# Dropping the empty slots' rows from the experts' indirect transfers, and adding their results to the residual by accumulating transfers on GpSimd's queue

## The chip, the cores and the metric

The kernel runs on one core of one Trainium2 chip. The metric is device time in microseconds (us) of one execution; lower is better. The engines are called PE (TensorE, matrix products), PEld (its weight loads), DVE (VectorE), ACT (ScalarE), POOL (GpSimd) and SP (SyncE, which here only issues transfers). SPq and POOLq are the queues of transfers that SP and POOL issue.

## The reference

Two blocks of layers run one behind the other on a sequence of 256 tokens of 1024 numbers. The change lies in one layer of the first block, a mixture of eight experts of which each token takes two:

```python
N_EXPERTS = 8
TOP_K = 2
D_FF_EXPERT = 7 * D_MODEL // 2
...
def moe_swiglu(xn, router, w_gu, w_down):
    logits = (xn @ router).astype(jnp.float32)
    top_v, top_i = lax.top_k(logits, TOP_K)
    w = jax.nn.softmax(top_v, axis=-1)
    comb = jnp.sum(jax.nn.one_hot(top_i, N_EXPERTS, dtype=jnp.float32) * w[..., None],
                   axis=-2).astype(xn.dtype)
    out = jnp.zeros_like(xn)
    for e in range(N_EXPERTS):
        out = out + comb[..., e:e + 1] * swiglu(xn, w_gu[e], w_down[e])
    return out
```

The layer's result is added to the residual: `h = h + moe_swiglu(rmsnorm(h, od_norm_moe[i]), od_router[i], ...)`. All tensors are float32.

## The kernel before

Weights come from DRAM in units of 1 MB (128 x 2048 float32, four blocks of 128 x 512). SP issues each as one transfer into one of four buffers `raw`. ACT casts each half to a rounded form `wh` (line 395), DVE forms the rest `wl = raw - wh` (line 396), and PE multiplies with both parts (line 372), three products for each block: `xh*wh`, `xl*wh`, `xh*wl`. There are five buffers of `wh` and four of `wl`, each half a unit. SP issues the next unit when DVE is through with the oldest `raw`. A unit is twelve products of 128 x 512, and the program is written in a fixed order; a tile framework's scheduler orders each engine's queue and sets the semaphores.

An expert holds 128 slots. Token t that goes to expert e has the slot that is its rank among the expert's tokens, so slots are filled from 0 upward (`pick` compares the rank with an iota). 256 tokens with two experts each make 512 filled slots of 8 x 128 = 1024: half are empty on average. A second pass for experts with more than 128 tokens stands in a branch and isn't taken here.

For expert e (`expert`, line 1260) the rows of its tokens are gathered from DRAM by slot (`slots`, an indirect transfer of 128 rows of 4 KB into `mo_got`, line 1245), transposed on PE and split (`turn`). Seven steps j follow, each of two products (gate, up), of 8 blocks each; ACT's `ff_s` at line 1281 stands once in each step, behind the gate's product. Two halves n of the down product follow, of 28 blocks each. Each half is scaled by the token's weight into `mo_y` (line 1294) and written by an indirect transfer of 128 rows of 2 KB to a DRAM tensor `results[n]` (named `mo_res`, line 1295): row t for a token whose first choice the expert is, row 256 + t for a second choice, and a spare row 512 + slot for an empty slot. `clear_results` sets the first 512 rows to zero early in the program. An empty slot's gather index is 0.

The last expert's results don't take that way: they are multiplied back to token order on PE and added to the residual `res` by DVE (line 1305). Ahead of that the other seven experts' results are collected (`collect`, at steps j = 2 and 3 of the last expert): for each half n and each choice w, SP loads 256 rows of 2 KB into `mo_z` (line 1326) and POOL adds them to `res` (line 1329, two instructions of 128 x 512 each, eight in all).

POOL runs its queue in order, the issuing of its transfers included.

Of the kernel before, what the change touches and what calls it, by code (L numbers as in the profile page):

```python
# [7 lines left out]
F32 = mybir.dt.float32  # L8
# [8 lines left out]
S = 256  # L17
# [6 lines left out]
TAPS_PE = 20  # L24
POOL_WINDOWS = (2, 4, 8, 16)
HQ = 64

# [65 lines left out]
def prep(i):  # L93
# [109 lines left out]
    slot = 2 * S + np.arange(128, dtype=np.float32)  # L203
    a["spare"] = np.stack([slot, -slot], axis=1)
    a["bigrows"] = np.ascontiguousarray(np.stack([f["final_norm"], f["od_norm_moe"][0], f["od_pw2_b"][0]]))

    p = np.arange(128)
# [96 lines left out]
class Build:  # L304
# [909 lines left out]
    def slot_tables(self, e):  # L1214

        nc = self.nc
        v = nc.vector
        P = self.picked  # L1220
        cws, rws, cw = self.slot_factors(e, P, self.moe_state[2])
        if e < NE - 1:
            to = self.sm(1, "mo_to")
            f = self.sm(NE + 1, "mo_to")
            v.tensor_copy(f, cw[:, NE + 2:])
            v.scalar_tensor_tensor(to, f[:, :1], self.spare[:, 1:2], f[:, 1 + e:2 + e], ALU.mult, ALU.add)
            back = self.sm(1, "mo_tx", I32)
            v.tensor_tensor(back, to, self.spare[:, 0:1], ALU.add)
        else:
            tr = self.scp(256)  # L1230
            for b in range(2):
                self.tp(tr[:, b * 128:b * 128 + 128], P[:, b])
            back = self.keep(S, "mo_PT", F32R)
            nc.scalar.copy(back, tr)
        return back, cws, rws, cw[:, NE + 1:NE + 2]

    def slots(self, e):


        nc = self.nc  # L1240
        back, cws, rws, at = self.slot_tables(e)
        ix = self.sm(1, "mo_ix", I32)
        nc.vector.tensor_copy(ix, at)
        got = self.sm(D, "mo_got")
        nc.gpsimd.indirect_dma_start(got, None, self.moe_state[1], bass.IndirectOffsetOnAxis(ap=ix.bitcast(U32), axis=0))
        return got, back, cws, rws

    def turn(self, slots):
# [11 lines left out]
    def expert(self, e, rest, then=None):  # L1260
# [29 lines left out]
        for n in range(2):  # L1290
            py, = self.ts(xh, xl, "moe_down", base + n * DFE * 512, DFE // 128, nb=1)
            if not then:
                y = self.sm(512, "mo_y")
                nc.scalar.activation(y, py, AF.Copy, scale=cws)
                nc.gpsimd.indirect_dma_start(self.results[n], bass.IndirectOffsetOnAxis(ap=back.bitcast(U32), axis=0), y, None)
                continue
            yh = self.sm(512, "mo_yh", F32R)
            yl = self.sm(512, "mo_yl", F32R)
            self.split_gain(yh, yl, py, cws)
            for b in range(2):  # L1300
                po = self.scp(512)
                self.mm(po, back[:, b * 128:b * 128 + 128], yh, True, False)
                self.mm(po, back[:, b * 128:b * 128 + 128], yl, False, True)
                r = self.res[b][:, n * 512:n * 512 + 512]
                v.tensor_tensor(r, po, r, ALU.add)
            then.half(n)

    def clear_results(self):
# [2 lines left out]
        nc = self.nc  # L1311
        zero = self.sm(512, "mo_zero")
        nc.gpsimd.memset(zero, 0.0)
        self.results = [self.dram.tile([2 * S + 128, 512], F32, name=f"mo_res{n}") for n in range(2)]
        for y in self.results:
            nc.scalar.dma_start(y[:2 * S].rearrange("(a p) d -> p a d", p=128), zero.unsqueeze(1).to_broadcast([128, 4, 512]))

        self.spare = self.keep(2, "mo_sp")
        nc.sync.dma_start(self.spare, self.A["spare"])

    def collect(self, n):

        nc = self.nc
        for w in range(2):
            z = self.sm((2, 512), "mo_z")
            nc.sync.dma_start(z, self.results[n][w * S:w * S + S].rearrange("(b p) d -> p b d", p=128))
            for b in range(2):
# [772 lines left out]
```

## Time and profile before

| | |
|---|---|
| time, median of 3 runs | 2287.48 us (2286.06 to 2288.99) |
| time of the profiled execution | 2284.27 us |
| its span, first to last instruction | 2282.4 us |
| mean granted TensorE clock | 0.999 |
| busy: PE, PEld, DVE, ACT, POOL | 2252.5, 1935.2, 1798.6, 1444.3, 115.1 us |
| bytes moved, mean rate | 588.63 MB, 258 GB/s |

The profiled execution lies 3.2 us (0.14%) below the median of the runs; about 1.9 us of it lie outside its span. Busy time of PE counts matrix products whose ends are modelled, so a high share doesn't say that PE runs at its peak. The eight experts run from about 616 us to 1611 us of the span.

### The profile page before, as it was taken

What the parts mean: (1) busy time and instruction counts of PE and PEld (TensorE: products, weight loads), DVE (VectorE), ACT (ScalarE), POOL (GpSimd) and SP (SyncE); (2) the same over time, 40 slices, a digit from 0 to 9 for tenths busy, and PEclk for the clock granted to TensorE, in tenths of its full rate; (3) what the DMA queues carried; (4) which work ended last, traced back from release to release, by engine and by line L of the source; (5) the groups of instructions that cost most, each with busy time, mean ns of one, the idle gap of its engine ahead of it and who ended that gap; (6) DMA issues with size and microseconds to landing.
All of it is one profiled execution on the core that took longest, in us unless ns stands there. A gap on an engine that the chain in (4) does not pass through costs nothing.

```text
span 2282.4 us, 34629 instructions
## 1 busy us (share of the span) xinstructions
PE 2252.5 (99%) x13069; PEld 1935.2 (85%) x13069; DVE 1798.6 (79%) x2601; ACT 1444.3 (63%) x2005; POOL 115.1 (5%) x163
## 2 busy tenths in 40 slices
PE   8999999999999999999999999989999999999999
PEld 8999998888878788888788878867788998888997
DVE  7656656986698898889898989888877885876883
ACT  5555545466567777777777777767765544665542
POOL 2100001301000000000000000020000000000000
PEclk9999999999999999999999999999999999999999
DMA  7544755954599989999999999989623555513553
GB/s 280 194 152 166 252 192 203 265 186 162 184 365 354 379 346 368 360 388 360 388 368 381 362 376 366 378 345 346 226 74 119 197 190 177 181 56 131 199 179 120
DMA packets 90891, 588.63 MB, mean 258 GB/s; under 512 B 11232, under 2 KB 12512, under 8 KB 24032
## 3 DMA queue, kind: packets, MB, share of 16 engines
q1 hardware_dynamic: 84752, 570.20, 67.7%
q0 software_dynamic: 4048, 12.97, 1.9%
q10 hardware_dynamic: 1920, 3.22, 0.4%
q8 instruction: 103, 1.69, 0.3%
q14 instruction: 68, 0.56, 0.1%
HBM read 577.31 MB, written 9.04 MB: 257 GB/s over the span
## 4 chain that ended last, share of the span: by engine, by line
PE 64%; DMA 4%; DVE 3%; ACT 1%; issue 1%; POOL 0%; ACTq 0%; DVEq 0%; POOLq 0%
PE acc L372 59%; DMA raw<-in_moe_gu_dram 3%; PE tr L376 3%; DVE wl L396 2%; PE sc L372 2%; ACT wh L395 1%; DMA raw<-in_moe_down_dram 0%; DMA ahead<-in_moe_gu_dram 0%; PE tr L372 0%; DVE res L556 0%; DVE xl L400 0%; POOL res L2043 0%; ACT at_p L1805 0%; DVE ff_s L1282 0%; DVE at_nm L1801 0%
## 5 line engine op out<-in xcount | busy, mean ns | idle before, releaser
L396 DVE TENSOR_TENSOR wl<-raw,wh 128x1024 fp32r<-128x1024 f32 x1054 | 1258.0, 1227 | 305.1 <-PE acc L372 176.9
L395 ACT CAST wh<-raw 128x1024 fp32r<-128x1024 f32 x1054 | 1060.1, 1047 | 431.5 <-PE acc L372 342.0
L372 PE MATMUL acc<-wh,mo_g 128*128 128x512 f32 x1568 | 488.8, 393 | 2.4 <-ACT wh L395 2.4
L372 PE MATMUL acc<-xl,wh 128*128 128x256 f32 x1440 | 399.1, 277 | 3.3 <-DVE xl L400 3.3
L372 PE MATMUL acc<-xh,wh 128*128 128x256 f32 x1440 | 399.7, 279 | 0.9 <-ACT xh L399 0.8
L372 PE MATMUL acc<-xh,wl 128*128 128x256 f32 x1440 | 398.0, 277 | 0.4 <-DVE wl L396 0.4
L372 PEld LDWEIGHTS acc<-wh,mo_g 128*128 128x128 f32 x1568 | 295.3, 189 | 64.8 <-ACT wh L395 3.5
L372 PE MATMUL acc<-wl,mo_g 128*128 128x512 f32 x784 | 314.8, 401 | 5.4 <-DVE wl L396 5.2
L372 PEld LDWEIGHTS acc<-xl,wh 128*128 128x128 f32 x1440 | 270.5, 188 | 5.2 <-DVE xl L400 4.5
L372 PEld LDWEIGHTS acc<-xh,wh 128*128 128x128 f32 x1440 | 270.0, 188 | 2.0 <-ACT xh L399 1.7
L372 PEld LDWEIGHTS acc<-xh,wl 128*128 128x128 f32 x1440 | 270.6, 188 | 0.6 <-DVE wl L396 0.6
L372 PEld LDWEIGHTS acc<-wl,mo_g 128*128 128x128 f32 x784 | 147.6, 188 | 49.4 <-DVE wl L396 21.4
L372 PE MATMUL acc<-wl,mhh 128*128 128x512 f32 x448 | 178.7, 399 | 2.4 <-DVE wl L396 1.6
L372 PE MATMUL acc<-wh,mhl 128*128 128x512 f32 x448 | 176.1, 393 | 0.0
L372 PE MATMUL acc<-wh,mhh 128*128 128x512 f32 x448 | 175.3, 391 | 0.0
L372 PEld LDWEIGHTS acc<-wl,mhh 128*128 128x128 f32 x448 | 84.2, 188 | 25.5 <-DVE wl L396 8.7
L372 PE MATMUL acc<-wl,hh 128*128 128x512 f32 x264 | 104.0, 394 | 0.0
L372 PE MATMUL acc<-wh,hl 128*128 128x512 f32 x264 | 103.5, 392 | 0.0
L372 PE MATMUL acc<-wh,hh 128*128 128x512 f32 x264 | 102.8, 390 | 0.0
L372 PEld LDWEIGHTS acc<-wh,mhl 128*128 128x128 f32 x448 | 84.1, 188 | 18.4
L372 PEld LDWEIGHTS acc<-wh,mhh 128*128 128x128 f32 x448 | 84.3, 188 | 17.2
L395 ACT CAST mhh<-tr 128x512 fp32r<-128x512 f32 x56 | 32.9, 588 | 94.8 <-PE tr L376 94.8
(439 smaller groups left out, 3103.8 us busy)
## 6 DMA issues: line engine op xcount, KB each, us to landing
raw<-in_moe_gu_dram SPq DMA_DIRECT2D x222, 1024.0 KB, 7.0
raw<-in_moe_down_dram SPq DMA_DIRECT2D x112, 1024.0 KB, 6.1
raw<-in_gu_dram SPq DMA_DIRECT2D x66, 1024.0 KB, 4.9
raw<-in_down_dram SPq DMA_DIRECT2D x30, 1024.0 KB, 4.8
raw<-in_w_in_b_dram SPq DMA_DIRECT2D x20, 1024.0 KB, 5.0
raw<-in_wkv_dram SPq DMA_DIRECT2D x16, 1024.0 KB, 5.0
raw<-in_pw_dram SPq DMA_DIRECT2D x12, 1024.0 KB, 4.8
raw<-in_wq_dram SPq DMA_DIRECT2D x8, 1024.0 KB, 4.8
```

What stands on the lines that cost most here:

```text
L372: self.nc.tensor.matmul(out, lhsT=l, rhs=r, start=start, stop=stop)
L376: self.nc.tensor.transpose(out, in_, self.ident[:n, :n])
L395: self.nc.scalar.copy(h, src)
L396: self.nc.vector.tensor_tensor(l, src, h.bitcast(F32), ALU.subtract)
```

## The change

The gather and the result writes get a bound: an index above it is skipped. An empty slot's index becomes 4096 (`PAST`) in both tables, so its row is neither read nor written; the spare rows of `mo_res`, the table `spare` and its load go away. DVE forms both indices in one pair of instructions, where it formed the write index in three and the gather index in one of its own. `collect` is called once, at step j = 0 of the last expert: eight transfers from DRAM on POOL's queue, each 128 rows of 2 KB, which the transfer itself adds to `res`. The loads into `mo_z` and POOL's eight additions go away.

```diff
+PAST = 4096.0
...
-    a["spare"] = np.stack([slot, -slot], axis=1)
...
         cws, rws, cw = self.slot_factors(e, P, self.moe_state[2])
+        f = self.sm(NE + 2, "mo_f")
+        v.tensor_copy(f, cw[:, NE + 1:])
         if e < NE - 1:
-            to = self.sm(1, "mo_to")
-            f = self.sm(NE + 1, "mo_to")
-            v.tensor_copy(f, cw[:, NE + 2:])
-            v.scalar_tensor_tensor(to, f[:, :1], self.spare[:, 1:2], f[:, 1 + e:2 + e], ALU.mult, ALU.add)
-            back = self.sm(1, "mo_tx", I32)
-            v.tensor_tensor(back, to, self.spare[:, 0:1], ALU.add)
...
+            to = self.sm(2, "mo_to")
+            v.scalar_tensor_tensor(to, f[:, 1:2].to_broadcast([128, 2]), -PAST, f[:, 0:3 + e:2 + e], ALU.mult, ALU.add)
+            ix = self.sm(2, "mo_tx", I32)
+            v.tensor_scalar(ix, to, PAST, None, ALU.add)
+            return ix[:, 1:2], cws, rws, ix[:, 0:1]
...
-        ix = self.sm(1, "mo_ix", I32)
-        nc.vector.tensor_copy(ix, at)
         got = self.sm(D, "mo_got")
-        nc.gpsimd.indirect_dma_start(got, None, self.moe_state[1], bass.IndirectOffsetOnAxis(ap=ix.bitcast(U32), axis=0))
+        nc.gpsimd.indirect_dma_start(got, None, self.moe_state[1], bass.IndirectOffsetOnAxis(ap=ix.bitcast(U32), axis=0),
+                                     bounds_check=S - 1, oob_is_err=False)
...
-            if e == NE - 1 and j in (2, 3):
-                self.collect(j - 2)
+            if e == NE - 1 and j == 0:
+                self.collect()
...
-                nc.gpsimd.indirect_dma_start(self.results[n], bass.IndirectOffsetOnAxis(ap=back.bitcast(U32), axis=0), y, None)
+                nc.gpsimd.indirect_dma_start(self.results[n], bass.IndirectOffsetOnAxis(ap=back.bitcast(U32), axis=0), y, None,
+                                             bounds_check=2 * S - 1, oob_is_err=False)
...
-    def collect(self, n):
...
-        for w in range(2):
-            z = self.sm((2, 512), "mo_z")
-            nc.sync.dma_start(z, self.results[n][w * S:w * S + S].rearrange("(b p) d -> p b d", p=128))
-            for b in range(2):
-                r = self.res[b][:, n * 512:n * 512 + 512]
-                nc.gpsimd.tensor_tensor(r, r, z[:, b], ALU.add)
...
+    def collect(self):
+
+        for n in range(2):
+            for w in range(2):
+                for b in range(2):
+                    r = self.res[b][:, n * 512:n * 512 + 512]
+                    row = (2 * w + b) * 128
+                    self.nc.gpsimd.dma_start(r, self.results[n][row:row + 128], accum_op=ALU.add)
```

POOL's queue at the change from the seventh expert to the last, before (`mo_res_2946` and `mo_res_2947` are the two halves n of the results, `res_69` and `res_70` the two row blocks of the residual):

```order
L1245 DMA mo_got<-mo_rows,mo_ix 128x1024
L1295 DMA mo_res_2946<-mo_y,mo_tx 640x512
L1295 DMA mo_res_2947<-mo_y,mo_tx 640x512
L1329 TENSOR_TENSOR res_69<-res_69,mo_z 128x512
L1329 TENSOR_TENSOR res_70<-res_70,mo_z 128x512
```

The four rows of line 1329 that follow, twice this pair and then another, read alike. The same place of POOL's queue in the changed kernel:

```order
L1244 DMA mo_got<-mo_rows,mo_tx 128x1024
L1295 DMA mo_res_2946<-mo_y,mo_tx 512x512
L1326 DMA res_69<-mo_res_2946 128x512
L1326 DMA res_70<-mo_res_2946 128x512
L1326 DMA res_69<-mo_res_2946 128x512
L1326 DMA res_70<-mo_res_2946 128x512
L1295 DMA mo_res_2947<-mo_y,mo_tx 512x512
L1326 DMA res_69<-mo_res_2947 128x512
L1326 DMA res_70<-mo_res_2947 128x512
L1326 DMA res_69<-mo_res_2947 128x512
L1326 DMA res_70<-mo_res_2947 128x512
```

Eight additions have become eight transfers. The four of the first half stand ahead of the seventh expert's second result write; the second choice's pair stands behind the first choice's and adds to the same tiles.

SP's queue over the last expert, before:

```order
L473 DMA raw<-in_moe_gu_dram 128x2048 x11
L1326 DMA mo_z<-mo_res_2946 128x2x512 x2
L473 DMA raw<-in_moe_gu_dram 128x2048 x5
L1326 DMA mo_z<-mo_res_2947 128x2x512 x2
L473 DMA raw<-in_moe_gu_dram 128x2048 x12
L473 DMA raw<-in_moe_down_dram 128x2048 x8
```

And in the changed kernel:

```order
L472 DMA raw<-in_moe_gu_dram 128x2048 x28
L472 DMA raw<-in_moe_down_dram 128x2048 x8
```

The four loads between the units of weights are gone; the units stand in the same order.

## Rows read from the trace of the kernel before

**Rows 1.** The page: the chain of work that ended last, shares by line

```profile
PE acc L372 59%; DMA raw<-in_moe_gu_dram 3%; PE tr L376 3%; DVE wl L396 2%; PE sc L372 2%; ACT wh L395 1%; DMA raw<-in_moe_down_dram 0%; DMA ahead<-in_moe_gu_dram 0%; PE tr L372 0%; DVE res L556 0%; DVE xl L400 0%; POOL res L2043 0%; ACT at_p L1805 0%; DVE ff_s L1282 0%; DVE at_nm L1801 0%
```

**Rows 2.** Stretch, its us, busy PE, PEld, DVE, ACT, POOL; clock, DMA, GB/s

```profile
837.00:958.00 121.00, 120.88 (x548) 97.99 (x546) 106.28 (x101) 90.85 (x103) 3.46 (x3) 1.00 0.94 360
1484.00:1525.00 41.00, 35.16 (x151) 26.25 (x150) 36.08 (x31) 26.29 (x30) 15.00 (x8) 1.00 0.94 363
1525.00:1530.00 5.00, 5.00 (x16) 3.90 (x16) 5.00 (x5) 3.07 (x4) 0.00 (x0) 0.68 0.61 223
660.00:716.00 56.00, 56.00 (x269) 45.73 (x268) 52.37 (x94) 40.78 (x48) 3.15 (x1) 1.00 0.94 347
```

**Rows 3.** Timeline of ACT over the last expert's steps (start, us)

```profile
1487.34 0.69 ACT L1281 ACTIVATE ff_s<-acc,mo_cw 128x512 f32<-128x512 f32 x1 [0.50 <-PE acc L372]
...
1498.84 0.69 ACT L1281 ACTIVATE ff_s<-acc,mo_cw 128x512 f32<-128x512 f32 x1 [0.50 <-PE acc L372]
1500.69 2.00 ACT L395 CAST wh<-raw 128x1024 fp32r<-128x1024 f32 x2 [1.16 <-DMA raw<-in_moe_gu_dram]
...
1513.12 0.69 ACT L1281 ACTIVATE ff_s<-acc,mo_cw 128x512 f32<-128x512 f32 x1 [0.49 <-PE acc L372]
...
1531.58 0.69 ACT L1281 ACTIVATE ff_s<-acc,mo_cw 128x512 f32<-128x512 f32 x1 [3.51 <-PE acc L372]
...
1543.08 0.69 ACT L1281 ACTIVATE ff_s<-acc,mo_cw 128x512 f32<-128x512 f32 x1 [0.51 <-PE acc L372]
```

**Rows 4.** Timeline of POOL over the experts

```profile
845.87 0.99 POOL L1295 DMA_INDIRECT mo_res<-mo_y,mo_tx  x1 [98.50 <-ACT mo_y L1294]
...
967.18 0.98 POOL L1295 DMA_INDIRECT mo_res<-mo_y,mo_tx  x1 [98.10 <-ACT mo_y L1294]
...
1087.99 0.98 POOL L1295 DMA_INDIRECT mo_res<-mo_y,mo_tx  x1 [98.76 <-ACT mo_y L1294]
...
1209.11 0.98 POOL L1295 DMA_INDIRECT mo_res<-mo_y,mo_tx  x1 [99.09 <-ACT mo_y L1294]
...
1329.37 0.98 POOL L1295 DMA_INDIRECT mo_res<-mo_y,mo_tx  x1 [98.21 <-ACT mo_y L1294]
...
1451.62 0.98 POOL L1295 DMA_INDIRECT mo_res<-mo_y,mo_tx  x1 [100.21 <-ACT mo_y L1294]
...
1496.83 8.00 POOL L1329 TENSOR_TENSOR res<-res,mo_z 128x512 f32<-128x512 f32 x4 [24.97 <-DMA mo_z<-mo_res]
1514.39 7.00 POOL L1329 TENSOR_TENSOR res<-res,mo_z 128x512 f32<-128x512 f32 x4 [9.56 <-DMA mo_z<-mo_res]
```

**Rows 5.** Timeline of DVE, 1484 to 1530 us

```profile
1489.00 4.63 DVE L396 TENSOR_TENSOR wl<-raw,wh 128x1024 fp32r<-128x1024 f32 x4 [0.72 <-ACT wh L395]
...
1497.41 4.03 DVE L396 TENSOR_TENSOR wl<-raw,wh 128x1024 fp32r<-128x1024 f32 x2 [0.25 <-ACT wh L395]
1501.77 6.41 DVE L396 TENSOR_TENSOR wl<-raw,wh 128x1024 fp32r<-128x1024 f32 x4 [0.33 <-ACT wh L395]
...
1514.78 4.23 DVE L396 TENSOR_TENSOR wl<-raw,wh 128x1024 fp32r<-128x1024 f32 x2 [0.71 <-ACT wh L395]
```

**Rows 6.** Transfers, 1347 to 1362 us: queue, packets, MB, share; landing

```profile
q0 software_dynamic: 224, 0.79, 13.0%
...
mo_res<-mo_y,mo_tx POOLq DMA_INDIRECT x1, 7.4
mo_got<-mo_rows,mo_ix POOLq DMA_INDIRECT x1, 10.7
```

**Rows 7.** Transfers, 1486 to 1500 us, the loads into mo_z among them

```profile
DMA packets 1161, 5.58 MB, mean 399 GB/s; under 512 B 96, under 2 KB 96, under 8 KB 608
```

**Rows 8.** Transfers, 256 to 272 us: queue of the zeros written to mo_res

```profile
q10 hardware_dynamic: 1056, 2.10, 34.2%
```

**Rows 9.** Instructions that write mo_ix: duration ns min/median/max

```profile
L1243 DVE CAST mo_ix<-sc x7: 152/154/158, 663.0 to 689.6; 128x1 int32<-128x1 f32 x7
```

**Rows 10.** The chain of work that ended last, 1580 to 1586 us

```profile
1582.79 0.19 DVE res L1305
```

More of the change, by code (lines that the diff above doesn't have):

```diff
@@ L202, in prep @@
     a["token"] = np.arange(S, dtype=np.float32).reshape(2, 128).T.copy()
-    slot = 2 * S + np.arange(128, dtype=np.float32)
-    a["spare"] = np.stack([slot, -slot], axis=1)
     a["bigrows"] = np.ascontiguousarray(np.stack([f["final_norm"], f["od_norm_moe"][0], f["od_pw2_b"][0]]))
@@ L1221, in slot_tables @@
         cws, rws, cw = self.slot_factors(e, P, self.moe_state[2])
+        f = self.sm(NE + 2, "mo_f")
+        v.tensor_copy(f, cw[:, NE + 1:])
         if e < NE - 1:
-            to = self.sm(1, "mo_to")
-            f = self.sm(NE + 1, "mo_to")
-            v.tensor_copy(f, cw[:, NE + 2:])
-            v.scalar_tensor_tensor(to, f[:, :1], self.spare[:, 1:2], f[:, 1 + e:2 + e], ALU.mult, ALU.add)
-            back = self.sm(1, "mo_tx", I32)
-            v.tensor_tensor(back, to, self.spare[:, 0:1], ALU.add)
-        else:
-            tr = self.scp(256)
-            for b in range(2):
[L1232 to L1235, printed above, removed]
+            to = self.sm(2, "mo_to")
[3 more added lines that the diff above has]
+            return ix[:, 1:2], cws, rws, ix[:, 0:1]
+        tr = self.scp(256)
+        for b in range(2):
+            self.tp(tr[:, b * 128:b * 128 + 128], P[:, b])
+        back = self.keep(S, "mo_PT", F32R)
+        nc.scalar.copy(back, tr)
+        ix = self.sm(1, "mo_tx", I32)
+        v.tensor_copy(ix, f[:, 0:1])
+        return back, cws, rws, ix
     def slots(self, e):
         nc = self.nc
-        back, cws, rws, at = self.slot_tables(e)
-        ix = self.sm(1, "mo_ix", I32)
-        nc.vector.tensor_copy(ix, at)
+        back, cws, rws, ix = self.slot_tables(e)
         got = self.sm(D, "mo_got")
-        nc.gpsimd.indirect_dma_start(got, None, self.moe_state[1], bass.IndirectOffsetOnAxis(ap=ix.bitcast(U32), axis=0))
+        nc.gpsimd.indirect_dma_start(got, None, self.moe_state[1], bass.IndirectOffsetOnAxis(ap=ix.bitcast(U32), axis=0),
+                                     bounds_check=S - 1, oob_is_err=False)
         return got, back, cws, rws
@@ L1313, in clear_results @@
         nc.gpsimd.memset(zero, 0.0)
-        self.results = [self.dram.tile([2 * S + 128, 512], F32, name=f"mo_res{n}") for n in range(2)]
+        self.results = [self.dram.tile([2 * S, 512], F32, name=f"mo_res{n}") for n in range(2)]
         for y in self.results:
-            nc.scalar.dma_start(y[:2 * S].rearrange("(a p) d -> p a d", p=128), zero.unsqueeze(1).to_broadcast([128, 4, 512]))
-        self.spare = self.keep(2, "mo_sp")
-        nc.sync.dma_start(self.spare, self.A["spare"])
-    def collect(self, n):
-        nc = self.nc
-        for w in range(2):
-            z = self.sm((2, 512), "mo_z")
-            nc.sync.dma_start(z, self.results[n][w * S:w * S + S].rearrange("(b p) d -> p b d", p=128))
-            for b in range(2):
-                r = self.res[b][:, n * 512:n * 512 + 512]
-                nc.gpsimd.tensor_tensor(r, r, z[:, b], ALU.add)
+            nc.scalar.dma_start(y.rearrange("(a p) d -> p a d", p=128), zero.unsqueeze(1).to_broadcast([128, 4, 512]))
+    def collect(self):
+        for n in range(2):
+            for w in range(2):
+                for b in range(2):
+                    r = self.res[b][:, n * 512:n * 512 + 512]
+                    row = (2 * w + b) * 128
+                    self.nc.gpsimd.dma_start(r, self.results[n][row:row + 128], accum_op=ALU.add)
     def angles(self):
```

## The prediction

> **What bounds the kernel now.** I read the chain of waits first. PE's products at line 372 hold 59% of the span on it, and the next entry is the landing of the experts' weights with 3% [rows 1]. So the kernel runs at PE's pace and loses time where weights come late. The table by stretches says where. In the second expert PE is busy 120.88 of 121 us while the transfer engines are busy 94% of the time at 360 GB/s: PE sets the pace and the transfers follow closely behind. [...]
>
> ACT's timeline gives the loss exactly, since `ff_s` stands once in each step, behind the gate's product. An undisturbed step is 11.5 us (1487.34 to 1498.84, 1531.58 to 1543.08). The two between take 14.28 and 18.46 us [rows 3]. They lose 2.8 + 7.0 = 9.7 us. This is where `collect` runs: POOL's additions start at 1496.83 and 1514.39 [rows 4].
>
> Two causes meet there. DVE's `wl` is slowed while POOL adds: four instructions in a row take 4.63 us undisturbed, but 6.41 at 1501.77, and pairs, about 2.3 us undisturbed, take 4.03 and 4.23. That is 1.8 + 1.7 + 1.9 = 5.4 us more [rows 5]. And the weights come late: ACT waits 1.16 us for a unit at 1500.69 [rows 3], behind the loads into `mo_z`, for which the queue has to move 2.1 MB more.
>
> A second, smaller loss is at the change of experts. The first result write of experts 1 to 6 stands at 845.87, 967.18, 1087.99, 1209.11, 1329.37 and 1451.62 [rows 4]: periods of 121.31, 120.81, 121.12, 120.26 and 122.25 us. Against the shortest they lose 1.05 + 0.55 + 0.86 + 0 + 1.99 = 4.45 us, 0.9 us each.
>
> **What the change removes.** POOL's eight additions and the `mo_z` loads go; with them the 9.7 us go, if nothing takes their place. Nothing else in the two steps differs from their neighbours: SP's queue holds the same units in the same order.
>
> **What the accumulating transfers cost.** They read the 2.1 MB that `mo_z` read, in rows of 2 KB. No accumulating transfer stands in the trace. The nearest row is the zeros written early on: 2.10 MB in 2 KB rows take 34.2% of 16 us, 5.5 us of all sixteen engines [rows 8]. I bound the accumulation from below by that, since the bytes must come once. A cost below it has no reason. From above I take twice, 11.0 us, since `res` has to be read as well as written. [...]
>
> When do they run? The first half waits for the seventh expert's first result write, issued at 1451.62 [rows 4] and landing 7.4 us later by its like [rows 6], so at about 1459. The second choice's pair adds to the same tiles and waits for the first pair, 7.4 to 10.7 us [rows 6]. The seventh expert's second result write stands behind the four on POOL's queue; POOL comes to it at about 1471, about when its data is ready (28 of an expert's 168 blocks behind the first: 120.26 x 28/168 = 20 us). The second half's pairs follow from about 1480, and all has landed near 1502. What is queued behind these waits on POOL are only the instructions at the layer's end; the first reader of the sums is DVE's addition at 1582.79 [rows 10]. So their latency is covered by 80 us, and only the transfer engines' time counts.
>
> How much of that is hidden? An expert needs 42 units, 44.0 MB. At the 399 GB/s that the engines reached when they were loaded most [rows 7] that is 110.4 us of the shortest period, 120.26 us: 8% is free, 3.5 us in the 43 us from 1459 to 1502. Prepared weights are a further cushion: at a change of experts a gather and a result write together take 13.0% of 15 us, 1.95 us [rows 6], and PE loses 0.9 us, so about 1.1 us is absorbed. Cover is thus 4.6 us. The accumulation costs PE 5.5 - 4.6 = 0.9 us at the lower end and 11.0 - 4.6 = 6.4 us at the upper. Neither end's row is nearer to an operation that reads two rows and writes one, so I take the middle, 3.6 us. Without the cover it would be 5.5 to 11.0.
>
> **What the skipped rows give.** Half of the slots are empty on average (512 filled of 1024). If the 1.95 us burst is halved, it falls below the cushion and at most 4.45 us come back; by bytes I would say half of the loss, 2.2 us. If the engines that carry the filled rows carry as much as before, nothing comes back. [...]
>
> **Edits that cost nothing.** DVE has five small instructions fewer; the gather's index cast was 154 ns each [rows 9]. They are done by about 690 us, in a stretch in which PE is busy 56.00 of 56 us [rows 2]; even uncovered they are under 1 us. The bound check adds an unknown time to POOL's issue of about 1 us per transfer [rows 4]; POOL idles some 98 us between them, and the gather is needed an expert later. Issuing eight transfers takes POOL about 8 us, where it worked 15 before. The missing load of `spare` and spare rows touch nothing that is waited for.
>
> **The sum.** 9.7 - 3.6 + 1.0 = 7.1 us less. The profiled execution, 2284.27 us, would become 2277.2. Runs of the kernel before have a median 3.2 us above it, and I carry that over: 2287.48 - 7.1 = 2280.4 us. A difference of 0.2%, 4.6 us, is about what a measurement of this kernel tells from none.
>
> **The rivals.**
> *The accumulation is as cheap as a copy.* POOL no longer slows DVE, and 0.9 us are left of the loss; the changes of experts give 1 to 3.5 us. For it: pairs go out apart, where `mo_z` came 1 MB at once. Gain 9.8 to 12.3, time 2275.2 to 2277.7 us.
> *The accumulation takes the place of the loads.* It costs 11 us or somewhat more, in a stage in which the transfer engines are busy 0.94 of the time anyway [rows 2], and starts nearly 40 us ahead of the additions of before, in the change from the seventh expert to the last. Together with no gain from skipped rows, or with rows that are skipped in name but still sent, the gain is 9.7 - 6.4 = 3.3 us or less, which can't be measured. Time 2283 to 2290 us.
> *Slower: an engine takes accumulating rows one at a time*, each with its reads, the addition and the write before the next. From 2.8 times a copy's time (15.3 us, less the cover 4.6, equals the 9.7 + 1.0 saved) the change loses; at 5 times, 27.5 - 4.6 - 10.7 gives 12.2 us more, 2299.7 us. Against it: sixteen engines share the rows, and transfers of 2 KB rows otherwise run at the full rate [rows 8].
>
> **How the numbers follow.** Forecast (gain 4.6 to 9 us): 36%, 2278.5 to 2282.9 us. Accumulation cheap (gain over 9): 27%. No difference within 0.2%: 25%. Slower by more: 12%. So faster 0.63, same 0.25, slower 0.12. The range from 2274.5 to 2288 us leaves out gains over 13 us (6%) and nearly all of the slower case together with the slow end of the equal one (14%).
>
> **What would show it.** POOL should have no busy time between 1484 and 1525 us, and no `wl` there should take over 1.3 us; if the slow ones remain, something else than POOL's additions slowed DVE. The steps of the last expert from 1475 on should exceed 11.5 us by 1 to 6 us in total, and the excess should lie ahead of 1497 us. The software queue's share of the transfer time over about 1459 to 1502 us gives the price of an accumulating row: 5.5 us or 11 us of sixteen engines, or far more. The software queue's packets per expert should be halved; if PE's loss at the changes of experts stays near 0.9 us all the same, the skipped rows gave nothing. If the last expert's loss is near 10 us again, the transfers alone made it, and the prediction is wrong in its main term.

## The result, and the profile after

| | before | changed |
|---|---|---|
| median, 5 runs each | 2287.48 us | 2299.73 us (2295.91 to 2301.95) |
| ratio, 95% interval | | 1.006, 1.0047 to 1.0072 |
| profiled execution | 2284.27 us | 2295.91 us |
| its span | 2282.4 us | 2294.1 us |
| mean granted clock | 0.999 | 0.999 |

The forecast was 2280.4 us, with a range of 2274.5 to 2288. The change makes the kernel 0.6% slower, outside the range.

The chain of work that ended last, shares by line, in the changed kernel (line numbers have moved by one to three):

```profile
PE acc L371 61%; PE tr L375 3%; PE sc L371 2%; DMA raw<-in_moe_gu_dram 2%; DVE wl L395 2%; DMA raw<-in_moe_down_dram 1%; ACT wh L394 1%; DMA ahead<-in_moe_gu_dram 0%; PE tr L371 0%; DVE res L555 0%; DVE xl L399 0%; POOL res L2040 0%; ACT at_p L1802 0%; DVE at_nm L1798 0%; DVE at_o L1842 0%
```

It reads like that of [rows 1]: PE's products hold 61% instead of 59%, and nothing new of 1% or more stands on it. So no large wait was added; the products themselves must hold the time. Before that is followed up, the experts. The first row is ACT's first `ff_s`, the second its last `mo_yh`, so the eight experts lie between; first before, then the changed kernel (start, us, engine):

```profile
624.49 0.69 ACT L1281 ACTIVATE ff_s<-acc,mo_cw 128x512 f32<-128x512 f32 x1
...
1604.16 0.69 ACT L399 ACTIVATE mo_yh<-acc,mo_cw 128x512 fp32r<-128x512 f32 x1 [0.90 <-PE acc L372]
```

```profile
633.06 0.69 ACT L1281 ACTIVATE ff_s<-acc,mo_cw 128x512 f32<-128x512 f32 x1
...
1605.86 0.69 ACT L398 ACTIVATE mo_yh<-acc,mo_cw 128x512 fp32r<-128x512 f32 x1 [0.97 <-PE acc L371]
```

The stage took 979.67 us and takes 972.80: 6.9 us less, nearly the 7.1 of the forecast. But the changed kernel comes to it 8.6 us late, and loses 10 us more behind it. I took each instruction of PE in both traces and the difference of its starts. It is -0.2 us at 201 us; grows evenly by 4.9 to 345 us (the first dense feed-forward layer); by 4.1 between 378 and 404; falls by 7.0 over the experts; grows by 4.5 from 1782 to 1916 us and by 4.9 from 2110 to 2256 (the second block's two feed-forward layers). 18.4 us are lost in four places that the diff doesn't touch.

The table by stretches shows three of them. The columns are us, then busy us and number of instructions of PE, PEld, DVE, ACT, POOL, then granted clock, DMA share, GB/s. Before:

```profile
230.00:310.00 80.00, 80.00 (x709) 80.00 (x707) 53.35 (x69) 39.44 (x48) 0.53 (x1) 1.00 0.64 234
1800.00:1860.00 60.00, 60.00 (x532) 60.00 (x531) 48.42 (x70) 29.16 (x34) 0.00 (x0) 1.00 0.57 194
2130.00:2190.00 60.00, 60.00 (x532) 60.00 (x531) 50.09 (x75) 28.99 (x33) 0.00 (x0) 1.00 0.57 195
```

The changed kernel:

```profile
230.00:310.00 80.00, 80.00 (x682) 80.00 (x681) 51.97 (x69) 38.99 (x47) 0.53 (x1) 1.00 0.62 227
1800.00:1860.00 60.00, 60.00 (x511) 60.00 (x511) 47.74 (x70) 28.83 (x34) 0.00 (x0) 1.00 0.55 190
2130.00:2190.00 60.00, 60.00 (x512) 60.00 (x511) 47.72 (x69) 28.83 (x34) 0.00 (x0) 1.00 0.55 190
```

PE and PEld are busy all the time in both, at a granted clock of 1.00, and the transfer engines are busy only 0.55 to 0.64 of the time, so they have room. The busy share, 80.00 of 80 us in both, can't show what is wrong; the count can. 709 products in 80 us are now 682, 532 in 60 us are now 511. From one start to the next it is 113.3 ns before and 117.8 ns now, for each product in these stretches. They are products of 256 columns, each with its own weight load; `xh` and `xl` move through PE, and `wh` and `wl` are loaded as its weights. In the experts a product has 512 columns and the roles are exchanged, and an undisturbed step is 11.5 us as before.

The fourth place is a meeting of DVE and POOL. First before, then the changed kernel, DVE's `wl` and POOL's addition of a bias row to the residual:

```profile
381.01 1.22 DVE L396 TENSOR_TENSOR wl<-raw,wh 128x1024 fp32r<-128x1024 f32 x1
...
381.05 6.23 POOL L942 TENSOR_TENSOR res<-res,brow 128x1024 f32<-128x1024 f32 x2 [150.45 <-PE tr L376]
```

```profile
385.76 3.42 DVE L395 TENSOR_TENSOR wl<-raw,wh 128x1024 fp32r<-128x1024 f32 x1
...
385.69 5.69 POOL L941 TENSOR_TENSOR res<-res,brow 128x1024 f32<-128x1024 f32 x2 [154.42 <-PE tr L375]
```

Before, `wl` started 0.04 us ahead of POOL and took 1.22 us. Now POOL starts 0.07 us ahead, and `wl` takes 3.42; POOL's two additions together get shorter, 6.23 to 5.69. DVE's `xl`, for which PE waits next, stands behind it and begins 6.1 us after that `wl` instead of 3.9. POOL's first addition ends at 388.10 us and `wl` 1.08 us behind it, at 389.18; by what means the one holds the other up, no run shows.

Behind that wait PE's clock fell in the changed kernel:

```profile
391.00:397.00 6.00, 4.63 (x28) 4.63 (x29) 3.22 (x5) 1.88 (x3) 1.04 (x5) 0.72 0.38 157
```

PE had been busy 5.63 of the 8 us from 383 to 391. The granted clock from 391 to 397 us is 0.72: cut into half microseconds it is 0.50 in each from 392 to 395, and 1.00 up to 391.5 and from 395.5 on; in the kernel before it is 1.00 from 386 to 392. By these rows I estimate at most 0.28 x 6 = 1.7 us for the clock; with 2.2 us more of waiting that is most of the 4.1.

What answers to the rows on the last expert, in the changed kernel. Table by stretches (the changed kernel is about 9 us late by then, so the stretch begins 9 us earlier in the program's course than that of [rows 2]):

```profile
1484.00:1525.00 41.00, 39.08 (x169) 29.62 (x168) 34.09 (x33) 29.69 (x33) 3.50 (x4) 1.00 1.03 382
```

POOL's timeline:

```profile
1456.94 1.01 POOL L1295 DMA_INDIRECT mo_res<-mo_y,mo_tx  x1 [98.93 <-ACT mo_y L1294]
1463.52 1.94 POOL L1326 DMA_DIRECT2D res<-mo_res  x2 [5.57 <-DMA mo_res<-mo_y,mo_tx]
1472.76 0.85 POOL L1326 DMA_DIRECT2D res<-mo_res  x1 [7.29 <-DMA res<-mo_res]
1476.55 0.88 POOL L1326 DMA_DIRECT2D res<-mo_res  x1 [2.95 <-DMA res<-mo_res]
1477.74 1.07 POOL L1295 DMA_INDIRECT mo_res<-mo_y,mo_tx  x1 [0.31 <-ACT wh L394]
1487.77 1.78 POOL L1326 DMA_DIRECT2D res<-mo_res  x2 [8.96 <-DMA mo_res<-mo_y,mo_tx]
1496.16 0.85 POOL L1326 DMA_DIRECT2D res<-mo_res  x1 [6.61 <-DMA res<-mo_res]
1499.98 0.87 POOL L1326 DMA_DIRECT2D res<-mo_res  x1 [2.96 <-DMA res<-mo_res]
```

ACT's `ff_s`:

```profile
1483.23 0.68 ACT L1281 ACTIVATE ff_s<-acc,mo_cw 128x512 f32<-128x512 f32 x1
...
1496.24 0.69 ACT L1281 ACTIVATE ff_s<-acc,mo_cw 128x512 f32<-128x512 f32 x1 [0.49 <-PE acc L371]
...
1510.15 0.68 ACT L1281 ACTIVATE ff_s<-acc,mo_cw 128x512 f32<-128x512 f32 x1
...
1521.92 0.69 ACT L1281 ACTIVATE ff_s<-acc,mo_cw 128x512 f32<-128x512 f32 x1 [0.52 <-PE acc L371]
```

DVE's `wl`:

```profile
1494.98 2.35 DVE L395 TENSOR_TENSOR wl<-raw,wh 128x1024 fp32r<-128x1024 f32 x2
...
1501.71 2.36 DVE L395 TENSOR_TENSOR wl<-raw,wh 128x1024 fp32r<-128x1024 f32 x2 [0.98 <-ACT wh L394]
...
1509.33 7.31 DVE L395 TENSOR_TENSOR wl<-raw,wh 128x1024 fp32r<-128x1024 f32 x6 [0.86 <-ACT wh L394]
```

PE is busy 39.08 of 41 us where it was 35.16 [rows 2]; POOL's 15 us are 3.5, all of it the issue of transfers. Pairs of `wl` take 2.35, six in a row 7.31: 1.22 each, no slow one is left [rows 5]. The steps take 13.01, 13.91 and 11.77 us: 4.2 us over three times 11.5, where 9.7 were lost [rows 3]. And what an accumulating transfer costs, the software queue's packets, MB and share of 16 engines' time from 1487 to 1510 us, the second half's four alone:

```profile
q0 software_dynamic: 578, 1.05, 24.7%
...
res<-mo_res POOLq DMA_DIRECT2D x4, 256.0 KB, 8.4
```

24.7% of 23 us is 5.7 us for 1.05 MB, 11.4 us for all eight: 2.07 times the 5.5 us of a copy [rows 8]. Those zeros went the other way, from SBUF to DRAM, but the loads that were replaced agree: in the kernel before, the 512 packets of 2 KB for `mo_z` from 1486 to 1500 us took 85 ns each, and the 512 packets of the accumulating transfers here took 176 ns each.

### The profile page after: what moved, and what is told of

Read it like the earlier page. It is cut to its first block, busy times and chain, and to the rows that moved or that the text cites. A ratio compares the mean times of both kernels' runs of the same rounds, so it can differ in the third digit from the quotient of the medians.

```text
span 2294.1 us, 34636 instructions
## 1 busy us (share of the span) xinstructions
PE 2267.0 (99%) x13069; PEld 1949.6 (85%) x13069; DVE 1794.5 (78%) x2596; ACT 1446.1 (63%) x2005; POOL 107.2 (5%) x163
## 4 chain that ended last, share of the span: by engine, by line
PE 66%; DMA 3%; DVE 2%; ACT 1%; issue 1%; POOL 0%; ACTq 0%; DVEq 0%; SPq 0%; POOLq 0%
PE acc L371 61%; PE tr L375 3%; PE sc L371 2%; DMA raw<-in_moe_gu_dram 2%; DVE wl L395 2%; DMA raw<-in_moe_down_dram 1%; ACT wh L394 1%; DMA ahead<-in_moe_gu_dram 0%; PE tr L371 0%; DVE res L555 0%; DVE xl L399 0%; POOL res L2040 0%; ACT at_p L1802 0%; DVE at_nm L1798 0%; DVE at_o L1842 0%
## 5 line engine op out<-in xcount | busy, mean ns | idle before, releaser
L371 PE MATMUL acc<-xl,wh 128*128 128x256 f32 x1440 | 404.9, 281 | 5.6 <-DVE xl L399 5.6
L371 PE MATMUL acc<-xh,wh 128*128 128x256 f32 x1440 | 405.5, 283 | 0.9 <-ACT xh L398 0.8
L371 PE MATMUL acc<-xh,wl 128*128 128x256 f32 x1440 | 403.5, 281 | 0.2 <-DVE wl L395 0.2
```

The costliest lines, as they stand in the source:

```text
L371: self.nc.tensor.matmul(out, lhsT=l, rhs=r, start=start, stop=stop)
```

## Experiments

Each ratio below is to runs of the kernel before on the same chip, whose medians were 2284.60 to 2285.97 us.

What could reach code that the diff doesn't touch? Not the transfers: they run from 670 us on, the loss begins at 201. The diff takes away one object that lies among the constants, the table `spare` (tile `mo_sp`, 8 bytes in each partition). The allocation of both programs, first byte of a buffer in each partition:

```
                              before   changed
mo_sp                          31424         -
part (first behind it)         31456     31424
xh, xl (first of 16 buffers)   69216     69184
wh (first of 5 buffers)       189600    189568
```

The table took 32 bytes, and each buffer behind it lies 32 bytes lower now. The 16 buffers of the activations and the five of `wh` are 4096 bytes each, so all of a class lie alike within 256 bytes. Theory A: that is the loss. Rival B: the missing load, or the new transfers.

### Both classes of buffers moved together

The kernel before with only the table put behind all other buffers; the instructions stay word for word:

```diff
-        self.spare = self.keep(2, "mo_sp")
+        self.spare = self.wp.tile([128, 2], F32, name="mo_sp", tag="mo_sp", bufs=1)
```

> The kernel before, with the 8-byte table spare taken out of its place among the constants and put behind the last buffer of the weights. Each instruction, transfer and order is that of before; only what was allocated behind the table lies 32 bytes lower, as in the changed kernel. Theory A (the changed kernel lost 18.6 us in code it doesn't touch because these buffers lie 32 bytes lower): slower than before by 15 to 19 us, about 2306 us, with the weight-stationary feed-forward products 281 ns instead of 276. Rival B (the missing load or the new transfers do it): same as before, 2287.5 us.

Measured: 2304.69 us, ratio 1.0077 (1.0062 to 1.0093).

```profile
230.00:310.00 80.00, 80.00 (x682) 80.00 (x681) 51.70 (x69) 38.73 (x48) 0.53 (x1) 1.00 0.62 224
1800.00:1860.00 60.00, 60.00 (x512) 60.00 (x511) 46.82 (x68) 27.66 (x32) 0.00 (x0) 1.00 0.55 187
2130.00:2190.00 60.00, 60.00 (x512) 60.00 (x511) 47.49 (x69) 28.09 (x33) 0.00 (x0) 1.00 0.55 186
```

The counts are those of the changed kernel, and the span, 2302.3 us, is 19.9 us longer. Theory A holds with no instruction changed. Not all 19.9 us are pitch: 1.9 stand ahead of 201 us, at a granted clock of 0.72 from 49 to 55 us, and 4.4 at the meeting of DVE and POOL, which here too falls as in the changed kernel (`wl` 3.43 us).

The other way round, the changed kernel with a constant where the table was, of n = 2, 16, 24 and 32 numbers, so that all behind it lies where it lay before, or 32, 64 and 96 bytes higher:

```diff
+        self.pad = self.keep(n, "mo_sp")
+        nc.gpsimd.memset(self.pad, 0.0)
```

> The changed kernel with a constant of 8 bytes put where spare stood, so that all buffers lie where they lay before; nothing reads it. Theory A (the addresses): the 18.6 us come back and the gain in the experts, 6.9 us, is left: 2281 us, near the forecast. Rival B (the missing load of spare or the new transfers themselves): 2299.7 us.

Measured: 2282.86 us, ratio 0.9989 (0.998 to 0.9998); its span is 2277.1, 5.2 us shorter than before.

```profile
230.00:310.00 80.00, 80.00 (x708) 80.00 (x708) 53.97 (x70) 40.07 (x48) 0.53 (x1) 1.00 0.65 236
1800.00:1860.00 60.00, 60.00 (x532) 60.00 (x531) 50.10 (x75) 29.22 (x35) 0.00 (x0) 1.00 0.57 194
2130.00:2190.00 60.00, 60.00 (x532) 60.00 (x531) 48.53 (x70) 28.97 (x33) 0.00 (x0) 1.00 0.57 196
```

The counts are back, and the loss of 4.1 us at 378 us is gone too. Against before, PE's starts differ by at most 2.2 us up to 1477 us, fall behind by up to 4.3 at 1500 us, and lead by 2.3 from 1530, by 5.0 from 1558 us and by 5.2 at the end. That is what the change itself does in these two executions. The profiled one here is the fastest of its eleven runs; by medians on the same chip, 2285.97 and 2282.86 us, the gain is 3.1 us.

> As the run with the 8-byte constant, but 64 bytes: the buffers lie 32 bytes higher than before, at multiples of 64 as in the changed kernel. Theory A with a 64-byte rule: slow, about 2300 us. A with a rule of 128 bytes or more, or of another kind: anything between 2281 and 2300. Rival B: 2299.7 us.

Measured: 2289.77 us, 1.0016 (1.0006 to 1.0025). The first two stretches:

```profile
230.00:310.00 80.00, 80.00 (x681) 80.00 (x681) 51.27 (x69) 38.92 (x48) 0.53 (x1) 1.00 0.63 226
1800.00:1860.00 60.00, 60.00 (x532) 60.00 (x531) 50.03 (x76) 29.24 (x34) 0.00 (x0) 1.00 0.56 193
```

A mixture: the first layer slow, both later ones fast. A plain rule of 64 bytes, which would have given about 2300 us, is refuted.

> As before it, but 96 bytes: the buffers lie 64 bytes higher than before, again at odd multiples of 32. Theory A with a 64-byte rule: fast, 2281 us. If each address but that of before is bad: about 2300. Rival B: 2299.7 us.

Measured: 2287.23 us, 1.0004 (0.9994 to 1.0014). All three stretches are fast (709, 532, 532); the meeting with POOL fell the bad way and cost 4.0 us again, with `wl` at 3.44 us. Another 3.0 us were lost just ahead of the experts, where the granted clock is 0.50 from 610 to 616 us. So this run says that the places give the fast pitch back, and not that they give the whole time back.

> The changed kernel with a constant of 128 bytes where spare stood: activations and weights together 96 bytes higher than before, that is 128 higher than in the changed kernel, at multiples of 64. If the common shift counts within 128 bytes: all three feed-forward stretches at 117.8 ns as in the changed kernel and about 2299 us. If within 256 or more: at least one stretch at 113.3 ns and 2282 to 2295 us, as with the constant of 64 bytes (2289.8 us). If only distances counted: 113.3 ns throughout and 2281 us.

Measured: 2300.38 us, 1.0058 (1.0044 to 1.0071), with 682, 512 and 512 products. So with both classes moved together, beginnings at odd multiples of 32 bytes gave 113.3 ns in all three stretches; beginnings at multiples of 64 gave 117.8 in all three at two places (the changed kernel's and 128 above it) and in one of three at the place between.

### One class moved against the other

Between the activations' buffers and the weights' a further pool of n numbers; for the first run the table itself goes there, so that the activations sink and the weights stay:

```diff
             self.small = pool("small")
+            self.gap = pool("gap")
...
+        pad = self.gap.tile([128, n], F32, name="pad", tag="pad", bufs=1)
+        nc.gpsimd.memset(pad, 0.0)
```

(In the runs with the 8-byte constant the last two lines are one.)

> The kernel before, with spare moved between the activations' buffers and the weights': activations (and the constants behind spare) 32 bytes lower, weights raw, wh, wl where they were. If the place of the moving operand xh, xl sets PE's pitch: 117.8 ns in the three feed-forward stretches and 14 us or more slower. If the place of the weights sets it: 113.3 ns, as before or up to 5 us slower. If neither alone does it but the start of each stretch falls one way or the other by small shifts in time: a mixture, some stretches at either pitch.

Measured: 2317.18 us, 1.0144 (1.0128 to 1.016).

> The kernel before, with 32 bytes put between the activations' buffers and the weights': the weights raw, wh, wl lie 32 bytes higher, at multiples of 64, all else as before. If the place of the weights sets PE's pitch: 117.8 ns in the three feed-forward stretches and 14 us or more slower. If that of the activations does: 113.3 ns, as before or up to 5 us slower. If the start of each stretch falls either way: a mixture.

Measured: 2317.39 us, 1.0139 (1.0121 to 1.0157).

Neither class's own place decides: either move costs about 32 us, and now the experts' steps suffer too, 11.64 instead of 11.50 us. What the two runs have in common is the distance between the classes, 32 bytes more than before. Each run moves a whole class, `raw` with `wh` and `wl`, or the activations with the constants; that the two operands PE reads are what counts is the nearest reading and was not tried apart. Further distances, on the changed kernel with the 8-byte constant:

> The changed kernel with the 8-byte constant, and the weights' buffers 64 bytes higher against the activations'. Theory A (32 bytes between the two classes cost 32 us because only their distance in steps of 64 counts): as without the gap, 2279 to 2287 us, or up to 2300 where a stretch falls to 117.8 ns. Rival B (each distance but that of before is slow): all stretches at 117 ns or more and 2310 us or more.

Measured: 2320.6 us, 1.0146 (1.0127 to 1.0164). Steps of 64 bytes aren't alike; theory A as I had put it for this run failed, and its rival's numbers came.

> As the last, with a gap of 96 bytes: an odd multiple of 32 again. Theory A: slow everywhere as with 32 bytes, an expert's step 11.64 us instead of 11.50, all products of 256 columns at 117 ns or more, 2308 to 2316 us. If only a distance of 32 bytes is bad: 2279 to 2300 us.

Measured: 2326.51 us, 1.0176 (1.0158 to 1.0193).

> As the last, with a gap of 448 bytes: the weights' buffers then lie at the same place as the activations' within each 512 bytes. Theory A (steps of 64 bytes are alike): 2279 to 2300 us as with the gap of 64. If a larger step counts, for instance equal places collide: another pitch than 113.3 or 117.8 ns in the three feed-forward stretches.

Measured: 2301.26 us, 1.006 (1.0045 to 1.0074).

> The changed kernel with the 8-byte constant and the weights' buffers 128 bytes higher against the activations'. If the pattern repeats after 128 bytes: 113.3 ns in the feed-forward stretches and steps of 11.50 us, 2279 to 2287 us. If after 256 or 512: 118 to 120 ns and 2300 to 2326 us.

Measured: 2314.38 us, 1.0128 (1.0112 to 1.0144).

> As the last with 256 bytes. If the pattern repeats after 256 bytes (or 128): 113.3 ns and 2279 to 2287 us. If after 512 or more: 116 to 120 ns and 2295 to 2326 us.

Measured: 2281.24 us, 0.9983 (0.9974 to 0.9992).

> As the last with 480 bytes, 32 less than 512. If the pattern repeats after 512 bytes and the pitch grows with the distance (113.3 at none, 117.3 at 32, 118.7 to 120.0 at 64): 110 to 113 ns, faster than before, 2265 to 2282 us. If instead only the distance of before is good: 117 to 120 ns and 2300 us or more.

Measured: 2314.7 us, 1.013 (1.0115 to 1.0145).

> The changed kernel with the 8-byte constant and the weights' buffers 160 bytes higher against the activations', the one distance of eight within 256 bytes that has not run. Theory (the pattern of seven: only the distance of before is good): 117 to 120 ns, 2300 to 2326 us. Rival (the distances 160 bytes up and 0 are a pair): 113.3 ns and about 2281 us.

Measured: 2309.78 us, 1.0106 (1.0091 to 1.0121).

In one table, by the distance from `xh` to `wh`, less whole multiples of 256. The count is that of the first stretch, 230 to 310 us; the pitch is the mean there from the start of one product to the next; the step is the shortest of the last expert's last three:

| distance | gap | products | pitch, ns | step, us |
|---|---|---|---|---|
| 0 | 448 | 669 | 120.0 | 11.43 |
| 32 | 480 | 679 | 118.3 | 11.62 |
| 64 | none | 708 | 113.3 | 11.48 |
| 64 | 256 | 708 | 113.3 | 11.48 |
| 96 | 32 (weights moved) | 685 | 117.3 | 11.64 |
| 96 | 32 (activations moved) | 676 | 118.7 | 11.63 |
| 128 | 64 | 669 | 120.0 | 11.58 |
| 160 | 96 | 669 | 120.0 | 11.66 |
| 192 | 128 | 682 | 117.8 | 11.63 |
| 224 | 160 | 688 | 116.7 | 11.62 |

With the gap of 256 bytes all is as with none. Only this distance was run twice so, so that the pattern repeats after 256 bytes is shown for it alone. In the two later stretches both runs at 96 have 117.2 to 117.3 ns. In all rows but one the activations lie where they lay before; how these distances do at another common place wasn't tried.

For products of 256 columns the kernel before lay at the one good distance of eight. The experts' products of 512 columns do as well at 0, with a step of 11.43 against 11.48 us. The change kept the distance and moved both, which at this distance is the smaller trap. Of the expectations, the gap of 96 was slow as its theory said, but slower than its 2308 to 2316 us; the hope of a pitch under 113 ns at 480 failed.

### The change's own parts, with the buffers where they were

Only the accumulating transfers (the new `collect` in the kernel before):

> The kernel before with only the new collect (eight accumulating transfers at step 0 of the last expert); slots, their indices and all buffers' places are those of before. The run with the 8-byte constant is 5.2 us shorter in its span than before, all of it between 760 and 1530 us. Theory A (the whole gain is the last expert's, the skipped rows give nothing): 4.5 to 6 us in the span, the last expert's steps as with the 8-byte constant (7.4, 13.4, 13.4, 12.0 us). Rival (skipped rows give 2 to 4 us): only 1 to 3 us shorter than before.

Measured: 2280.91 us, 0.9987 (0.9977 to 0.9996); span 2276.2, 6.2 us shorter than before. The first `ff_s` to the last `mo_yh` takes 974.3 us.

Only the skipped rows (the changed kernel with the 8-byte constant and the old `collect`):

> The changed kernel with the 8-byte constant in spare's place and the old collect (loads into mo_z, POOL's additions): only the skipped rows are left of the change. Theory A: as before within 1.5 us, since the run with the moved table, which skips nothing, lost no more at the changes of experts (11.44 to 11.62 us a step) than the changed kernel. Rival: 2 to 4 us shorter, and the last expert's steps 14.3 and 18.5 us as before.

Measured: 2282.18 us, 0.9991 (0.9981 to 1.0001); span 2276.6, stage 973.5. The rival came nearer than theory A, but the interval holds both. The last expert's steps are 14.26 and 16.41 us, 2.1 us less than before, though its additions are those of before: from 1490 to 1540 us the granted clock is 1.00 here, and 0.97 in the kernel before, where it fell at the end of the longer step [rows 2]. So 2.1 us of this run's gain lie here and not at the changes of experts, where the skipped rows were to save.

Each part alone shows as much as both together (973.7 us), and the kernel with the moved table, which has neither, 978.5. The three profiled executions with 8 bytes in the old place are each the fastest of their runs; medians on the same chip say the same, 4.2 us less than before for the transfers alone, 2.9 for the skipped rows alone and 3.1 for both. The two don't add up; how they share the gain stays open.

Then the place of the transfers. First by moving the calls of `collect`, a pair each at steps 2, 3, 4 and 5:

```diff
-            if e == NE - 1 and j == 0:
-                self.collect()
+            if e == NE - 1 and j in (2, 3, 4, 5):
+                self.collect(*divmod(j - 2, 2))
...
```

> The changed kernel with the 8-byte constant in spare's place, and the accumulating transfers issued a pair at a time at steps 2, 3, 4 and 5 of the last expert instead of all at step 0. Theory A (each accumulating row costs transfer time that the weights lack; spread over four steps of 11.5 us most of it is hidden): the steps of the last expert lose under 2 us together instead of 4.3, and the span is 2 to 5 us shorter than with all eight at step 0 (2277.1 us). Rival (the cost is a fixed one for each transfer, wherever it stands): the loss moves to steps 2 to 5 and stays 4 us or more.

Measured: 2280.95 us, 0.9974 (0.9964 to 0.9984); steps 13.04, 13.89 and 11.77 us. It tested neither: POOL issued the transfers at 1456.82 to 1494.02 us all the same, since nothing on POOL's queue stood ahead of them and no data held them back. So a dependence was made, ahead of one transfer at each step:

```diff
+        r = self.res[b][:, n * 512:n * 512 + 512]
+        if s is not None:
+            self.nc.vector.scalar_tensor_tensor(r[:, :1], s[:, :1], 0.0, r[:, :1], ALU.mult, ALU.add)
+        row = (2 * w + b) * 128
+        self.nc.gpsimd.dma_start(r, self.results[n][row:row + 128], accum_op=ALU.add)
```

> The changed kernel with the 8-byte constant, and each accumulating transfer held back to a step of its own: ahead of the transfer for step j DVE adds zero times one element of the last step's ff_s to the first column of the piece of the residual that the transfer adds to, which leaves the sum as it is. One transfer at each of the steps 0 to 5, two at step 6. Theory A (transfer time that the weights lack at the start of the last expert is the cost): the steps of the last expert lose under 1.5 us together instead of 4.3, and the median is 2 to 4 us below that of the changed kernel with the constant (2282.9, or 0.9989 of before). Rival (a fixed cost for each transfer): the loss is spread over the steps and stays 4 us or more.

Measured: 2275.45 us (2273.91 to 2276.39), ratio 0.9958 (0.9946 to 0.997). POOL's timeline, ACT's steps, and the software queue from 1483 to 1550 us:

```profile
1457.68 1.00 POOL L1329 DMA_DIRECT2D res<-mo_res  x1 [5.92 <-DMA mo_res<-mo_y,mo_tx]
...
1483.14 0.90 POOL L1329 DMA_DIRECT2D res<-mo_res  x1 [11.64 <-DVE res L1327]
1494.17 0.87 POOL L1329 DMA_DIRECT2D res<-mo_res  x1 [10.13 <-DVE res L1327]
1505.73 0.87 POOL L1329 DMA_DIRECT2D res<-mo_res  x1 [10.68 <-DVE res L1327]
1518.36 0.85 POOL L1329 DMA_DIRECT2D res<-mo_res  x1 [11.76 <-DVE res L1327]
1529.76 0.86 POOL L1329 DMA_DIRECT2D res<-mo_res  x1 [10.55 <-DVE res L1327]
1541.94 1.74 POOL L1329 DMA_DIRECT2D res<-mo_res  x2 [11.32 <-DVE res L1327]
```

```profile
1474.86 0.69 ACT L1282 ACTIVATE ff_s<-acc,mo_cw 128x512 f32<-128x512 f32 x1 [0.77 <-PE acc L371]
...
1486.72 0.69 ACT L1282 ACTIVATE ff_s<-acc,mo_cw 128x512 f32<-128x512 f32 x1 [0.51 <-PE acc L371]
...
1498.29 0.69 ACT L1282 ACTIVATE ff_s<-acc,mo_cw 128x512 f32<-128x512 f32 x1 [0.50 <-PE acc L371]
...
1509.78 0.69 ACT L1282 ACTIVATE ff_s<-acc,mo_cw 128x512 f32<-128x512 f32 x1 [0.51 <-PE acc L371]
...
1521.95 0.69 ACT L1282 ACTIVATE ff_s<-acc,mo_cw 128x512 f32<-128x512 f32 x1 [0.53 <-PE acc L371]
...
1533.99 0.69 ACT L1282 ACTIVATE ff_s<-acc,mo_cw 128x512 f32<-128x512 f32 x1 [0.54 <-PE acc L371]
...
1545.58 0.69 ACT L1282 ACTIVATE ff_s<-acc,mo_cw 128x512 f32<-128x512 f32 x1 [0.53 <-PE acc L371]
```

```profile
q0 software_dynamic: 960, 1.77, 15.4%
```

The transfers cost about as much: 15.4% of 67 us is 10.3 us for 1.77 MB, 5.8 us for each MB against 5.4 with all at step 0. But the six steps lose 0.36 + 0.07 + 0 + 0.67 + 0.54 + 0.09 = 1.7 us instead of 4.2, just over theory A's 1.5 and far from the rival's 4. So the cover is longer at nearly the same price. Here the transfers also go out one at a time, but for the last two, where at step 0 two ran at once; which of the two helps wasn't tried apart. This version beats both kernels: each of its six runs is faster than each of the kernel before, and the ratio is 0.4% below 1. Against the changed kernel with the constant its span is 3.2 us shorter, as theory A had it; by the two ratios it would be some 7 us, which the steps don't explain.

## Why the prediction was wrong

**The step that failed** is the last of the edits that cost nothing: "The missing load of `spare` and spare rows touch nothing that is waited for." The load indeed doesn't; but the table's 32 bytes set where each buffer behind it begins, and with it the pitch of PE's products in some 420 us of other layers, 4.9 + 4.5 + 4.9 = 14.3 us. With the places came the meeting of DVE and POOL, 4.1 us. All of it was costed at nothing and is worth 17 to 20 us: 2299.73 against 2282.86 us with the 8-byte constant, and 19.9 us of span for the kernel before with the table moved. The order of the instructions, from which I argued, shows no place in memory. The sum took for granted that the rest of the program keeps its time.

**POOL and DVE**: right. Without the additions no `wl` is slow, and the 9.7 us are gone. As a size it is less firm than it looked: with the same loads and additions the last expert lost 10.1 us in the kernel with the moved table and 7.6 in the one with skipped rows alone.

**The accumulating transfers**: that they cost PE time was right, the size was off. I took the middle of 5.5 and 11.0 us, and the engines' time is 11.4, just above the upper end: twice a copy, as the prediction's upper end had it for reading and writing `res`; what the engines do in that time no run shows apart. With 4.6 us of cover this would have been 6.8 us lost. Measured are 4.2 in the last expert's steps and, ahead of them, at most 3 us more: from the seventh expert's first `ff_s` to the last expert's it takes 122.5 to 123.5 us in the seven kernels at the distance of before with the call at step 0 (125.1 with the calls moved), against 120.3 to 122.6 in three without. That they end near 1502 us was right: the last lands at 1508.4 in a kernel that is about 9 us late by then. That the excess lies ahead of 1497 us came only in part: 1.5 us fall in the step that ends at 1496.24, 2.4 in the next, which ends at 1510.15, some 1501 by the course of before.

**The skipped rows**: the traffic is halved, what PE has of it is open. The software queue (packets, MB, share) over the first six experts, before from 624 to 1353 us, then the changed kernel from 633 to 1360:

```profile
q0 software_dynamic: 1744, 6.03, 2.1%
```

```profile
q0 software_dynamic: 1773, 3.10, 1.1%
```

2.1% of 729 us is 15.3 us of all engines, 1.1% of 727 is 8.0. The count of packets stays: those of 4 KB fell from 1472 to 753, and in place of the others stand packets of 4 or 8 bytes, 9 ns each. The periods of experts 2 to 6, counted from 1, add up to 602.2 to 604.1 us in three kernels at the distance of before without skipping, and to 601.4 to 605.2 in nine with it. No run shows the 1.0 us that the sum has for it: that was my estimate, between nothing and the 2.2 us by bytes, and it lies within what these differ among themselves. Skipping alone in the run above gave 2.9 us by medians, with an interval that reaches to nothing. (The prediction's "second expert" and "experts 1 to 6" count from 0, its "seventh expert" from 1.)

**The sum** of the change alone: 5.2 us of span where I said 7.1. That the experts' stage in the changed kernel gained 6.9 us, so near to it, is in part luck: the transfers cost more than the 3.6 that I took, and the term of the skipped rows isn't measured. By medians it is 3.1 us, by the ratio 0.11%, with an interval that ends at 0.02%: too small to tell from no change by the measure I had set.

**The rivals.** An accumulation as cheap as a copy is refuted by 2.07. That it takes the place of the loads came near: its price was that rival's. The slower rival named 2299.7 us, which is what was measured, and for a wrong reason: it needed a price of 5 copies.

**What stays open.** Why PE's pitch depends on the distance of the two classes of buffers within 256 bytes, and why, at the good distance, the pair's place matters as well. The same two paces stand side by side at the good distance: behind a few products of another kind, PE's starts in the kernel before, from 204.27 us on, follow each other by 202, 122, 116, 114 and 113 ns and stay there; with the table moved, from 206.20 us on, by 200, 118, 118, 117 and 118, and stay there. Which pace these long stretches fall into was the same wherever the buffers lay alike: six kernels that have the places of before show the fast one in all three. Short stretches elsewhere can differ, as in the kernel before from 378.8 to 380.5 us, with 117 to 120 ns. Nothing here shows the mechanism. The loss at 378 us follows from a few hundredths of a microsecond between DVE and POOL. It goes with the places too, but not with the pitch: `wl` starts 0.03 to 0.04 us ahead of POOL in all seven kernels that have the places of before or the gap of 256, and 0.06 to 0.07 behind in all five in which both classes moved together, the fast one with 96 bytes among them. What turns it was not tried.

## What to carry to other kernels

An edit that adds or removes a buffer moves what is allocated behind it, here by 32 bytes that were worth 17 to 20 us; before a small difference is put down to the edit itself, run the old kernel with only the places changed, and the new one with the old places. Where PE is busy all the time in both traces, count its products in a stretch: here it was busy 80.00 of 80 us with 709 of them and with 682. And a transfer that only has to be done by some later time is worth holding back by a dependence and spreading over its slack: here the last expert's steps then lost 1.7 us instead of 4.2. Moving the calls in the program alone left the issues at 1456.82 to 1494.02 us, as nothing on POOL's queue stood ahead of them.

## What the runs showed of the hardware

- Products of 256 columns with a weight load each ran at 113.3 ns or at up to 120 ns for one, by the distance within 256 bytes between the buffers of the activations and those of the weights, at eight distances in steps of 32; the same program differed by 1.4% for 32 bytes. What makes the slow pitch, 116.7 ns and more, no run here shows.
- At the good distance two paces, 113.3 and 117.8 ns, hold for a whole long stretch; a common shift of 32 bytes down turned one into the other in three of three stretches, 32 bytes up in one of three.
- An accumulating transfer into SBUF in rows of 2 KB took 2.07 times the engines' time of a copy of the same bytes, 176 against 85 ns for a packet of 2 KB.
- Where rows were skipped by the bound, packets of 4 or 8 bytes and 9 ns each were left; with about half of the rows skipped the engines' time for the gathers and result writes of six experts fell from 15.3 to 8.0 us.
- DVE's subtraction of 128x1024 took 1.22 or 3.42 us, as it began 0.04 us ahead of POOL's addition or 0.07 us behind; behind the longer wait PE's granted clock was 0.72 over the 6 us from 391 to 397.
